# First value weights on ScalarE's DMA queue, norm rows in two tiles, constants after the first weights, rotary sines after the value projection

## The chip, the cores and the metric

The kernel runs on one core of a Trainium2 chip. The metric is the device time of one execution, in microseconds (us). The engines of the core run side by side and meet at semaphores: TensorE (PE), VectorE (DVE), ScalarE (ACT), GpSimd (POOL) and SyncE (SP, which here only starts DMA transfers). ScalarE and GpSimd can start DMA transfers too.

## What is computed

Two decoder layers over 256 positions of 1024 channels. Layer 0 mixes tokens by attention (8 heads of 128, rotary embedding on 32 of the 128 channels of a head, one block of 256 keys, so plain causal attention), layer 1 by causal pooling with windows 2, 4, 8 and 16. Each layer is followed by a squared-ReLU MLP of width 4096, and one RMSNorm ends the program. Cut to the part that the change touches:

```python
def rms_norm(x, g):
    return x * rsqrt(mean(x * x, axis=-1) + 1e-6) * g

xn = rms_norm(x, norm_mix[0])
q, k, v = split(xn @ w_qkv)                  # 8 heads of 128
q, k = rope(q, cos, sin), rope(k, cos, sin)  # on 32 of the 128 channels
p = softmax(q @ k.T / sqrt(128) + causal)
x = x + (p @ v) @ w_o
x = x + relu(rms_norm(x, norm_mlp[0]) @ w_up) ** 2 @ w_down
```

## The kernel before

All of x stays on the chip in `xt`. Every weight arrives as float32 in a slab of 1 MB (`raw_*`, three buffers) and is split into two parts, a high one (`wh_*`, ScalarE, L160) and the rest (`wl_*`, VectorE, L164); the activations are split likewise (`xs`, high half by ScalarE at L293, low half by VectorE at L299). A product is then three matmuls: high by high, low by high, high by low. A slab goes through the split in pieces of 512 or 1024 columns. The order of the engines' work is the order of the code: no scheduler moves anything. `pump(n)` writes n pieces of the next slab's split into the queues of ScalarE and VectorE at the place where it stands in the code; `use(...)` writes what is still missing of the slab that is needed. The load of a slab is issued on SyncE when the last piece of the slab three before it has been split (L167).

The start of the program, in the order in which TensorE sees it: eight matmuls on a zero tile (`warm`, L270, each recorded as two), the transposition of the 32 rows of the two norms' gains (`gps`, L274, copied to `gcol` by VectorE, L276), the transposition of the first 128 channels of x (`tr_a`, L287), two more zero matmuls, and then the value projection (`d_v`, L461), eight steps k of 12 matmuls with the transpositions of the later channels between them. Behind it come `rb` (L502), which spreads the inverse root mean square over the partitions, and four rounds j of: k projection (`u_k`), q projection (`u_q`), scores of the round before (`s`, L539 and L540), its softmax, its product with the values.

Beside that, GpSimd computes the rotary angles from the positions (L417 to L426, 18 instructions), VectorE brings them into range (`last_turn`, L429 to L432), ScalarE takes two sines (`sines`, L435 and L436, between two table loads), GpSimd forms the cosines (L438, L439), and VectorE multiplies both with `rb` into four tables (L508, L509). After each projection of round j VectorE swaps the rotary halves (`sw_k`, `sw_q`, L522) and multiplies by the cosines (`t_k`, `t_q`, L523), and GpSimd multiplies the swapped part by the sines (L524) and adds it (L525). The scores of a round wait for L525 of its q.

ScalarE's Sqrt of the mean square (`aerr`, L479) and VectorE's steps L482 to L491 behind it give `arst` and `diag`, which `rb` and the values' copies (`vsb`, L497) need. The queues of DMA: x and all weights on SyncE's; the two norms' rows (`grow`) on ScalarE's; `inv` and `pos_i`, which the rotary angles start from, on GpSimd's.

Of the kernel before, what the change touches and what calls it, by code (L numbers as in the profile page):

```python
# [11 lines left out]
F32 = mybir.dt.float32  # L12
# [29 lines left out]
N_WARM2 = 2  # L42
# [41 lines left out]
def tile_trunk(ctx: ExitStack, tc: tile.TileContext, x_in, positions, norm_mix, norm_mlp,  # L84
# [136 lines left out]
    tiny = cpool.tile([P, 1], F32, name="tiny")  # L221
    nc.scalar.activation(tiny, warm[:, 0:1], AF.Sqrt)
# [7 lines left out]
    grow = cpool.tile([32, P], F32, name="grow")  # L230
# [9 lines left out]
    def load_v0(eng, k, h):  # L240
        eng.dma_start(v0[:, k, h * HALF:(h + 1) * HALF], v0_src[:, k, h * HALF:(h + 1) * HALF])

    load_x(0, 1)
    nc.scalar.dma_start(grow[0:16, :], norm_mix.rearrange("l (k p) -> (l k) p", p=P))
    nc.scalar.dma_start(grow[16:32, :], norm_mlp.rearrange("l (k p) -> (l k) p", p=P))
    load_v0(nc.sync, 0, 0)
    load_v0(nc.sync, 0, 1)
    load_x(1, 1)
    load_v0(nc.sync, 1, 0)
    load_v0(nc.sync, 1, 1)  # L250
    load_x(2, 2)
    load_to(1)
    load_x(4, 4)
    inv = cpool.tile([ROT, 1], F32, name="inv")
    nc.gpsimd.dma_start(inv, consts[0:ROT, C_INV:C_INV + 1])
    pos_i = cpool.tile([ROT, SEQ], I32, name="pos_i")
    nc.gpsimd.dma_start(pos_i, positions.broadcast_to([ROT, SEQ]))
    cst = cpool.tile([P, C_ALL], F32, name="cst")
    load_to(RAW_BUFS - 1)
    nc.sync.dma_start(cst, consts)  # L260
# [12 lines left out]
    gps = ps_t.tile([P, HALF], F32, tag="t", name="gps")  # L273
    nc.tensor.transpose(gps[:, 0:32], grow, ident[0:32, 0:32])  # L274
    gcol = cpool.tile([P, 32], F32, name="gcol")
    nc.vector.tensor_copy(gcol, gps[:, 0:32])  # L276
# [167 lines left out]
    h, lo = transposes(0, 0, "a", n=1)  # L444
    keep_warm(N_WARM2)
# [4 lines left out]
    for k in range(KT):  # L450
# [12 lines left out]
        pump(2 if k < 3 or k == 6 else 1)  # L463
# [7 lines left out]
        if k == 6:  # L471
            sines()
        if k == 5:
            var0 = small.tile([P, NS], F32, tag="avar", name="avar", bufs=1)
            r0t = small.tile([P, NS], F32, tag="arst", name="arst", bufs=1)
            e0 = small.tile([P, NS], F32, tag="aerr", name="aerr", bufs=1)
            nc.vector.scalar_tensor_tensor(var0, acc0[:, 0, :], EPS, acc0[:, 1, :],
                                           op0=ALU.add, op1=ALU.add)
            nc.scalar.activation(e0, var0, AF.Sqrt)  # L479
            pump_h(1)  # L480
            last_turn()
            nc.vector.reciprocal(r0t, e0)  # L482
            nc.vector.tensor_tensor(e0, var0, r0t, op=ALU.mult)
            nc.vector.tensor_tensor(e0, e0, r0t, op=ALU.mult)
            nc.vector.tensor_scalar(e0, e0, -0.5, 1.5, op0=ALU.mult, op1=ALU.add)
            nc.vector.tensor_tensor(r0t, r0t, e0, op=ALU.mult)
            r0 = [r0t[:, s:s + 1] for s in range(NS)]
            diags = []
            for s in range(NS):
                diag = small.tile([P, P], F32, tag="diag%d" % s, name="diag%d" % s, bufs=1)  # L490
                nc.vector.tensor_scalar(diag, ident, r0[s], None, op0=ALU.mult)  # L491
                diags.append(diag)

# [11 lines left out]
    for nm, c in (("k", 1.0), ("q", scale)):  # L505
        ct = cpool.tile([P, 1, SEQ], F32, name="ct_" + nm)
        st = cpool.tile([ROT, 1, SEQ], F32, name="st_" + nm)
        nc.vector.scalar_tensor_tensor(ct[:, 0, :], rb[:, 0:SEQ], c, cos_t, op0=ALU.mult, op1=ALU.mult)  # L508
        nc.vector.scalar_tensor_tensor(st[:, 0, :], rb[0:ROT, 0:SEQ], c, sin_t, op0=ALU.mult, op1=ALU.mult)  # L509
        tab[nm] = (ct, st)  # L510
# [82 lines left out]
    for j in range(4):  # L593
# [12 lines left out]
        if j == 0:  # L606
            v_evac(0, 1)
            v_evac(1, 1)
        qk["k", j] = qk_evac("k", j, u)
# [365 lines left out]
```

## Time and profile before

| | before |
|---|---|
| median of 3 runs | 494.3 us (493.9 to 494.57) |
| the profiled execution, its own time | 494.89 us |
| its span in the profile | 493.1 us |
| TensorE matmul busy | 481.9 us, 98% of the span |
| VectorE, ScalarE, GpSimd busy | 333.1, 249.7, 50.2 us |

A row of the timeline gives the start and the length in us, the engine, the line, the operation, and what it writes and reads, with the count if rows were merged; in brackets stands how long the engine had been idle before it and what ended that. The records of neighbouring instructions on one engine overlap by up to 0.3 us, so what an instruction costs its engine is the distance from its start to the next start.

### The profile page before, as it was taken

How to read it: one execution, taken by the hardware profiler on the slowest of the kernel's cores; microseconds unless marked ns; L12 is line 12 of the kernel's file. 1: busy time of each engine (PE TensorE's matmuls, PEld its weight loads, DVE VectorE, ACT ScalarE, POOL GpSimd, SP SyncE). 2: the span in 40 equal slices, each digit the busy share in tenths (PEclk: the TensorE clock that was granted, in tenths of full speed). 3: DMA queues.
4: the chain of work that ended last, by engine and by line, in shares of the span. 5: the costliest groups of instructions: out<-in, count | busy, mean ns of one | idle time of the engine just before them, and what ended most of it. 6: DMA issues, size and time to landing. Idle time of an engine off the chain costs nothing.

```text
span 493.1 us, 6591 instructions
## 1 busy us (share of the span) xinstructions
PE 481.9 (98%) x2625; PEld 416.2 (84%) x2625; DVE 333.1 (68%) x484; ACT 249.7 (51%) x395; POOL 50.2 (10%) x46
## 2 busy tenths in 40 slices
PE   9999999999999999999999999999999999999993
PEld 7789899888888888888888889888888888888882
DVE  3788788765867866666666676678666666655645
ACT  4776444563665644444455553566444554445423
POOL 6935534200000000000000000000000000000000
PEclk9999999999999999999999999999999999999998
DMA  7949435471396656565554580077765555566102
GB/s 269 384 160 291 157 105 171 129 241 58 96 345 213 242 185 202 208 215 210 174 171 171 170 256 1 7 251 240 265 212 178 172 170 173 187 201 229 66 0 85
DMA packets 56078, 89.53 MB, mean 182 GB/s; under 512 B 1600, under 2 KB 44640, under 8 KB 56048
## 3 DMA queue, kind: packets, MB, share of 16 engines
q1 hardware_dynamic: 55632, 88.68, 53.8%
q8 instruction: 20, 0.33, 0.3%
q10 hardware_dynamic: 352, 0.41, 0.2%
q14 instruction: 10, 0.08, 0.0%
q0 software_dynamic: 64, 0.03, 0.0%
HBM read 88.06 MB, written 1.05 MB: 181 GB/s over the span
## 4 chain that ended last, share of the span: by engine, by line
PE 84%; POOL 5%; DVE 5%; ACT 2%; issue 2%; DMA 1%; POOLq 0%; ACTq 0%; DVEq 0%
PE u_m L381 24%; PE u_m L375 12%; PE d_m L352 11%; PE d_m L351 11%; PE d_m L353 11%; POOL rot_b L425 2%; PE d_o L353 1%; PE d_o L351 1%; PE d_o L352 1%; PE u_q L365 1%; PE u_q L360 1%; PE u_q L361 1%; POOL rot_a L426 1%; DMA raw_k<-in_attn_w_qkv_dram 1%; POOL sw_q L524 1%
## 5 line engine op out<-in xcount | busy, mean ns | idle before, releaser
L381 PE MATMUL u_m<-xs,wh_u 128*128 128x512 f32 x512 | 129.8, 395 | 0.0
L381 PEld LDWEIGHTS u_m<-xs,wh_u 128*128 128x128 f32 x512 | 91.8, 188 | 16.6
L352 PE MATMUL d_m<-wl_d,hh 128*128 128x512 f32 x256 | 99.9, 390 | 0.0
L351 PE MATMUL d_m<-wh_d,hh 128*128 128x512 f32 x256 | 99.9, 390 | 0.0
L353 PE MATMUL d_m<-wh_d,hl 128*128 128x512 f32 x256 | 99.6, 389 | 0.0
L164 DVE TENSOR_TENSOR wl_d<-raw_d,wh_d 128x1024 fp32r<-128x1024 f32 x64 | 77.8, 1224 | 23.3 <-ACT wh_d L160 23.3
L666 ACT ACTIVATE t<-u_m 128x256 f32<-128x256 f32 x64 | 24.4, 381 | 108.7 <-PE u_m L381 108.6
L164 DVE TENSOR_TENSOR wl_u<-raw_u,wh_u 128x1024 fp32r<-128x1024 f32 x64 | 75.5, 1219 | 1.8 <-ACT wh_u L160 1.8
L375 PEld LDWEIGHTS u_m<-xs,wl_u 128*128 128x128 f32 x512 | 70.0, 188 | 5.4
L375 PE MATMUL u_m<-xs,wl_u 128*128 128x256 f32 x512 | 72.7, 283 | 0.0
L160 ACT ACTIVATE wh_d<-raw_d 128x1024 fp32r<-128x1024 f32 x64 | 66.5, 1048 | 3.7 <-DMA raw_d<-in_mlp_w_down_dram 3.6
L667 DVE TENSOR_TENSOR t<-u_m,t 128x256 f32<-128x256 f32 x64 | 27.1, 424 | 56.8 <-ACT t L666 56.8
L160 ACT ACTIVATE wh_u<-raw_u 128x1024 fp32r<-128x1024 f32 x64 | 63.9, 1045 | 0.0
L351 PEld LDWEIGHTS d_m<-wh_d,hh 128*128 128x128 f32 x256 | 48.0, 188 | 10.6
L352 PEld LDWEIGHTS d_m<-wl_d,hh 128*128 128x128 f32 x256 | 48.1, 188 | 10.2
L353 PEld LDWEIGHTS d_m<-wh_d,hl 128*128 128x128 f32 x256 | 48.1, 188 | 10.2
L677 ACT ACTIVATE hh<-hf 128x512 fp32r<-128x512 f32 x32 | 20.2, 632 | 47.3 <-DVE hf L676 47.3
L678 DVE TENSOR_TENSOR hl<-hf,hh 128x512 fp32r<-128x512 f32 x32 | 22.2, 693 | 22.5 <-ACT hh L677 22.5
L676 DVE SCALAR_TENSOR_TENSOR hf<-t 128x512 f32<-128x512 f32 x32 | 22.2, 694 | 1.1
L360 PE MATMUL u_q<-xs,wh_q 128*128 128x256 f32 x64 | 18.6, 291 | 0.0
L360 PE MATMUL u_k<-xs,wh_k 128*128 128x256 f32 x64 | 18.5, 289 | 0.0
L365 PE MATMUL u_k<-xs,wh_k 128*128 128x256 f32 x64 | 18.1, 283 | 0.0
(170 smaller groups left out, 578.9 us busy)
## 6 DMA issues: line engine op xcount, KB each, us to landing
raw_u<-in_mlp_w_up_dram SPq DMA_DIRECT2D x32, 1024.0 KB, 5.8
raw_d<-in_mlp_w_down_dram SPq DMA_DIRECT2D x32, 1024.0 KB, 6.4
raw_k<-in_attn_w_qkv_dram SPq DMA_DIRECT2D x4, 1024.0 KB, 5.2
raw_q<-in_attn_w_qkv_dram SPq DMA_DIRECT2D x4, 1024.0 KB, 5.2
raw_o<-in_attn_w_o_dram SPq DMA_DIRECT2D x4, 1024.0 KB, 5.2
raw_v<-in_attn_w_qkv_dram SPq DMA_DIRECT2D x3, 1024.0 KB, 9.3
raw_v<-in_attn_w_qkv_dram SPq DMA_DIRECT2D x4, 256.0 KB, 4.4
pw<-in_pool_w_dram SPq DMA_DIRECT2D x1, 1024.0 KB, 11.2
```

Source lines behind the costliest of these rows:

```text
L160: nc.scalar.activation(wh[:, sl], src[:, sl], AF.Copy)
L164: nc.vector.tensor_tensor(wl[:, sl], src[:, sl], wh[:, sl].bitcast(F32), op=ALU.subtract)
L351: nc.tensor.matmul(acc, lh, wh, start=first, stop=False)
L352: nc.tensor.matmul(acc, lh, wl, start=False, stop=False)
L353: nc.tensor.matmul(acc, ll, wh, start=False, stop=last)
L360: nc.tensor.matmul(o, w[0][:, k, fs], hi, start=first, stop=False, skip_group_check=True)
L365: nc.tensor.matmul(acc[:, f * SEQ:(f + 1) * SEQ], w[0][:, k, fs], xs[:, k, SEQ:2 * SEQ], start=False, stop=last, skip_group_check=True)
L375: nc.tensor.matmul(acc[:, 0:SEQ], w[1][:, k, f * P:(f + 1) * P], xs[:, k, 0:SEQ], start=k == 0, stop=False, skip_group_check=True)
L381: nc.tensor.matmul(acc, w[0][:, k, f * P:(f + 1) * P], xs[:, k, :], start=False, stop=k == KT - 1, skip_group_check=True)
L666: nc.scalar.activation(t[:, ts], u[:, SEQ:2 * SEQ], AF.Copy)
L667: nc.vector.tensor_tensor(t[:, ts], u[:, 0:SEQ], t[:, ts], op=ALU.add)
L676: nc.vector.scalar_tensor_tensor(hf, t, 0.0, t, op0=ALU.max, op1=ALU.mult)
```

## The change

The first quarter of the first value slab is loaded over ScalarE's DMA queue, ahead of the gains; the second half of that slab is one transfer instead of two, and the second slab is two transfers of half a slab instead of one. The gains of the two norms lie in two tiles of 16 rows: `grow` (mixer norm) is transposed behind the first x transposition, `grow2` (MLP norm) inside the value projection. `inv` and `pos_i` come over ScalarE's queue instead of GpSimd's. ScalarE's first table load stands behind these four transfers. The constants (`cst`) are loaded behind the slab of `k` instead of behind the third slab. `N_WARM2` is 7 instead of 2. `last_turn` and `sines` stand behind the value projection instead of within its steps 5 and 6, the tables (`tables()`) behind the second half of the first k projection, and step 7 of the value projection pumps two pieces instead of one.

```diff
-N_WARM2 = 2
+N_WARM2 = 7
...
-    tiny = cpool.tile([P, 1], F32, name="tiny")
-    nc.scalar.activation(tiny, warm[:, 0:1], AF.Sqrt)
...
-    grow = cpool.tile([32, P], F32, name="grow")
+    grow = cpool.tile([16, P], F32, name="grow")
+    grow2 = cpool.tile([16, P], F32, name="grow2")
...
     load_x(0, 1)
-    nc.scalar.dma_start(grow[0:16, :], norm_mix.rearrange("l (k p) -> (l k) p", p=P))
-    nc.scalar.dma_start(grow[16:32, :], norm_mlp.rearrange("l (k p) -> (l k) p", p=P))
-    load_v0(nc.sync, 0, 0)
+    load_v0(nc.scalar, 0, 0)
+    nc.scalar.dma_start(grow, norm_mix.rearrange("l (k p) -> (l k) p", p=P))
     load_v0(nc.sync, 0, 1)
     load_x(1, 1)
-    load_v0(nc.sync, 1, 0)
-    load_v0(nc.sync, 1, 1)
+    nc.sync.dma_start(v0[:, 1, :], v0_src[:, 1, :])
     load_x(2, 2)
-    load_to(1)
+    raw1 = rawp.tile([P, SLAB], F32, tag="raw", name="raw_v_1")
+    raws[1] = raw1
+    state["raw"] = 2
+    for k in range(2):
+        nc.sync.dma_start(raw1[:, k * D:(k + 1) * D], slabs[1][1][:, k, :])
+    inv = cpool.tile([ROT, 1], F32, name="inv")
+    nc.scalar.dma_start(inv, consts[0:ROT, C_INV:C_INV + 1])
+    pos_i = cpool.tile([ROT, SEQ], I32, name="pos_i")
+    nc.scalar.dma_start(pos_i, positions.broadcast_to([ROT, SEQ]))
+    tiny = cpool.tile([P, 1], F32, name="tiny")
+    nc.scalar.activation(tiny, warm[:, 0:1], AF.Sqrt)
     load_x(4, 4)
...
+    nc.sync.dma_start(grow2, norm_mlp.rearrange("l (k p) -> (l k) p", p=P))
...
-    nc.sync.dma_start(cst, consts)
...
-    gps = ps_t.tile([P, HALF], F32, tag="t", name="gps")
-    nc.tensor.transpose(gps[:, 0:32], grow, ident[0:32, 0:32])
-    nc.vector.tensor_copy(gcol, gps[:, 0:32])
+    def gains(src, c0):
+        gps = ps_t.tile([P, HALF], F32, tag="t", name="gps_%d" % c0)
+        nc.tensor.transpose(gps[:, 0:16], src, ident[0:16, 0:16])
+        nc.vector.tensor_copy(gcol[:, c0:c0 + 16], gps[:, 0:16])
...
     h, lo = transposes(0, 0, "a", n=1)
+    gains(grow, 0)
     keep_warm(N_WARM2)
...
-        pump(2 if k < 3 or k == 6 else 1)
+        pump(2 if k < 3 or k >= 6 else 1)
+        if k == 2:
+            load_to(3)
+            nc.sync.dma_start(cst, consts)
+        if k == 6:
+            gains(grow2, 16)
...
-        if k == 6:
-            sines()
...
-            last_turn()
...
+    last_turn()
+    sines()
...
+    def tables():
...
             v_evac(1, 1)
+            tables()
```

TensorE's queue at the start, before; `warm_up` is the target of the zero matmuls, `gps` that of the gains' transposition:

```order
L270 MATMUL warm_up<-warm 128x128 x8
L274 MATMUL gps<-ident,grow 128x32
L287 MATMUL tr_a_158<-ident,xt 128x128 x2
L270 MATMUL warm_up<-warm 128x128 x2
L461 MATMUL d_v_153<-wh_v_163,xs 128x512
```

The same place after:

```order
L273 MATMUL warm_up<-warm 128x128 x8
L293 MATMUL tr_a_155<-ident,xt 128x128 x2
L281 MATMUL gps_158<-ident,grow 128x16
L273 MATMUL warm_up<-warm 128x128 x7
L468 MATMUL d_v_150<-wh_v_168,xs 128x512
```

Seven zero matmuls instead of two stand between the first transpositions and the first matmul of the value projection.

ScalarE's queue behind the split of the first k slab, before (`wh_q` is the first q slab, the last `wh_k` the second k slab):

```order
L160 ACTIVATE wh_k_344<-raw_k_237 128x1024 x2
L435 ACT_TABLE_LOAD
L435 ACTIVATE sin_t<-rot_a 32x256
L436 ACTIVATE rot_b<-rot_a 32x256
L437 ACT_TABLE_LOAD
L437 ACTIVATE tiny<-warm 128x1
L160 ACTIVATE wh_q_372<-raw_q_282 128x1024 x2
L160 ACTIVATE wh_k_419<-raw_k_348 128x1024
```

And after:

```order
L160 ACTIVATE wh_k_346<-raw_k_242 128x1024 x2
L160 ACTIVATE wh_q_372<-raw_q_288 128x1024 x2
L441 ACT_TABLE_LOAD
L441 ACTIVATE sin_t<-rot_a 32x256
L442 ACTIVATE rot_b<-rot_a 32x256
L443 ACT_TABLE_LOAD
L443 ACTIVATE tiny<-warm 128x1
L160 ACTIVATE wh_k_420<-raw_k_350 128x1024 x2
```

The sines have moved behind the first q slab, and directly behind them stands the second k slab, with both of its pieces.

VectorE's queue from the tables to the first round's q, before:

```order
L508 SCALAR_TENSOR_TENSOR ct_q<-rb,cos_t 128x256
L509 SCALAR_TENSOR_TENSOR st_q<-rb,sin_t 32x256
L164 TENSOR_TENSOR wl_q_373<-raw_q_282,wh_q_372 128x1024
L164 TENSOR_TENSOR wl_k_420<-raw_k_348,wh_k_419 128x1024
L522 STREAM_SHUFFLE sw_k_452<-u_k_390 32x512
L523 TENSOR_TENSOR t_k_451<-u_k_390,ct_k 128x512
L164 TENSOR_TENSOR wl_k_420<-raw_k_348,wh_k_419 128x1024
L164 TENSOR_TENSOR wl_q_462<-raw_q_353,wh_q_461 128x1024 x2
L522 STREAM_SHUFFLE sw_q_519<-u_q_465 32x512
```

After, from the last instruction of `last_turn` on:

```order
L438 TENSOR_SCALAR rot_a<-rot_a 32x256
L164 TENSOR_TENSOR wl_k_421<-raw_k_350,wh_k_420 128x1024 x2
L521 SCALAR_TENSOR_TENSOR ct_k<-rb,cos_t 128x256
L522 SCALAR_TENSOR_TENSOR st_k<-rb,sin_t 32x256
L521 SCALAR_TENSOR_TENSOR ct_q<-rb,cos_t 128x256
L522 SCALAR_TENSOR_TENSOR st_q<-rb,sin_t 32x256
L535 STREAM_SHUFFLE sw_k_465<-u_k_395 32x512
L536 TENSOR_TENSOR t_k_464<-u_k_395,ct_k 128x512
L164 TENSOR_TENSOR wl_q_471<-raw_q_355,wh_q_470 128x1024 x2
L164 TENSOR_TENSOR wl_k_504<-raw_k_378,wh_k_503 128x1024
L535 STREAM_SHUFFLE sw_q_532<-u_q_478 32x512
```

The whole first q slab and `last_turn` now stand ahead of the second k slab, the tables stand behind it, and one piece of the third k slab (`wl_k_504`) stands ahead of `sw_q`.

## Rows read from the trace of the kernel before

**Rows 1.** Waits of TensorE, whole span: for whom, us, times, longest.

```profile
PE s L539 <- POOL t_q L525: 1.1, 1, 1.1
```

**Rows 2.** Timeline of TensorE, start to the first scores.

```profile
1.05 3.78 PE L270 MATMUL warm_up<-warm 128*128 128x128 f32 x16 [1.05 <-DVE warm L220]
...
5.49 0.64 PE L270 MATMUL warm_up<-warm 128*128 128x128 f32 x4
6.25 1.25 PE L461 MATMUL d_v<-wh_v,xs 128*128 128x512 f32 x4
...
13.32 1.20 PE L461 MATMUL d_v<-wh_v,xs 128*128 128x512 f32 x4 [0.51 <-ACT xs L293]
...
16.74 0.60 PE L287 MATMUL tr_a<-ident,xt 128*128 128x128 f32 x4
17.09 2.10 PE L461 MATMUL d_v<-wh_v,xs 128*128 128x512 f32 x8
...
22.76 0.60 PE L287 MATMUL tr_a<-ident,xt 128*128 128x128 f32 x4
...
31.97 0.61 PE L502 MATMUL rb<-diag,ones 128*128 128x128 f32 x4
...
51.06 0.49 PE L539 MATMUL s<-t_k,t_q 128*128 128x128 f32 x2 [1.15 <-POOL t_q L525]
```

**Rows 3.** Timeline of ScalarE, first weights to the second k slab.

```profile
4.47 0.63 ACT L160 ACTIVATE wh_v<-raw_v 128x512 fp32r<-128x512 f32 x1 [2.24 <-DMA raw_v<-in_attn_w_qkv_dram]
...
25.29 0.20 ACT L479 ACTIVATE aerr<-avar 128x2 f32<-128x2 f32 x1 [0.45 <-DVE avar L477]
...
29.65 0.42 ACT L435 ACTIVATE sin_t<-rot_a 32x256 f32<-32x256 f32 x1
...
31.80 2.00 ACT L160 ACTIVATE wh_q<-raw_q 128x1024 fp32r<-128x1024 f32 x2
36.06 1.06 ACT L160 ACTIVATE wh_k<-raw_k 128x1024 fp32r<-128x1024 f32 x1 [2.27 <-DMA raw_k<-in_attn_w_qkv_dram]
```

**Rows 4.** Timeline of VectorE, mean square to the first round's q.

```profile
25.06 0.19 DVE L477 SCALAR_TENSOR_TENSOR avar<-acc 128x2 f32<-128x2 f32 x1
27.01 0.28 DVE L429 TENSOR_SCALAR rot_b<-rot_a 32x256 f32<-32x256 f32 x1 [1.76 <-POOL rot_a L426]
...
28.30 0.15 DVE L482 RECIPROCAL arst<-aerr 128x2 f32<-128x2 f32 x1
...
29.67 1.22 DVE L164 TENSOR_TENSOR wl_v<-raw_v,wh_v 128x1024 fp32r<-128x1024 f32 x1
...
33.70 1.21 DVE L164 TENSOR_TENSOR wl_q<-raw_q,wh_q 128x1024 fp32r<-128x1024 f32 x1
34.83 0.41 DVE L508 SCALAR_TENSOR_TENSOR ct_k<-rb,cos_t 128x256 f32<-128x256 f32 x1
...
36.16 1.20 DVE L164 TENSOR_TENSOR wl_q<-raw_q,wh_q 128x1024 fp32r<-128x1024 f32 x1
...
40.42 1.23 DVE L164 TENSOR_TENSOR wl_k<-raw_k,wh_k 128x1024 fp32r<-128x1024 f32 x1 [0.68 <-ACT wh_k L160]
41.56 3.46 DVE L164 TENSOR_TENSOR wl_q<-raw_q,wh_q 128x1024 fp32r<-128x1024 f32 x2
...
44.95 0.73 DVE L522 STREAM_SHUFFLE sw_q<-u_q 32x512 f32<-32x512 f32 x1
...
46.18 2.34 DVE L164 TENSOR_TENSOR wl_k<-raw_k,wh_k 128x1024 fp32r<-128x1024 f32 x2
```

**Rows 5.** Timeline of GpSimd, its share in the first and third round's q.

```profile
45.76 3.91 POOL L524 TENSOR_TENSOR sw_q<-sw_q,st_q 32x512 f32<-32x512 f32 x1 [2.96 <-DVE sw_q L522]
49.75 1.26 POOL L525 TENSOR_TENSOR t_q<-t_q,sw_q 32x512 f32<-32x512 f32 x1
...
74.63 1.28 POOL L524 TENSOR_TENSOR sw_q<-sw_q,st_q 32x512 f32<-32x512 f32 x1 [5.05 <-DVE sw_q L522]
```

**Rows 6.** Stretch around the wait at 51.06: us, busy by engine, PEclk, DMA share, GB/s.

```profile
49.00:51.10 2.10, 0.95 (x9) 0.75 (x7) 1.06 (x3) 0.00 (x0) 2.02 (x3) 1.00 0.78 235
```

More of the change, by code (lines that the diff above doesn't have):

```diff
@@ L243, in tile_trunk @@
     load_x(0, 1)
-    nc.scalar.dma_start(grow[0:16, :], norm_mix.rearrange("l (k p) -> (l k) p", p=P))
-    nc.scalar.dma_start(grow[16:32, :], norm_mlp.rearrange("l (k p) -> (l k) p", p=P))
-    load_v0(nc.sync, 0, 0)
+    load_v0(nc.scalar, 0, 0)
+    nc.scalar.dma_start(grow, norm_mix.rearrange("l (k p) -> (l k) p", p=P))
     load_v0(nc.sync, 0, 1)
     load_x(1, 1)
-    load_v0(nc.sync, 1, 0)
-    load_v0(nc.sync, 1, 1)
+    nc.sync.dma_start(v0[:, 1, :], v0_src[:, 1, :])
     load_x(2, 2)
-    load_to(1)
+    raw1 = rawp.tile([P, SLAB], F32, tag="raw", name="raw_v_1")
[9 more added lines that the diff above has]
+    nc.scalar.activation(tiny, warm[:, 0:1], AF.Sqrt)
     load_x(4, 4)
[L254 to L257, printed above, removed]
+    nc.sync.dma_start(grow2, norm_mlp.rearrange("l (k p) -> (l k) p", p=P))
     cst = cpool.tile([P, C_ALL], F32, name="cst")
     load_to(RAW_BUFS - 1)
-    nc.sync.dma_start(cst, consts)
     psb = cpool.tile([P, D], F32, tag="psb", name="psb")
@@ L504, in tile_trunk @@
     tab = {}
[L505 to L510, printed above, removed]
+    def tables():
+        for nm, c in (("k", 1.0), ("q", scale)):
+            ct = cpool.tile([P, 1, SEQ], F32, name="ct_" + nm)
+            st = cpool.tile([ROT, 1, SEQ], F32, name="st_" + nm)
+            nc.vector.scalar_tensor_tensor(ct[:, 0, :], rb[:, 0:SEQ], c, cos_t, op0=ALU.mult, op1=ALU.mult)
+            nc.vector.scalar_tensor_tensor(st[:, 0, :], rb[0:ROT, 0:SEQ], c, sin_t, op0=ALU.mult, op1=ALU.mult)
+            tab[nm] = (ct, st)
     swap = [(i + half) % ROT for i in range(ROT)]
```

## Prediction

> **What bounds the kernel now.** I read the waits of TensorE first, because it is the engine that is busy nearly all the time. There the reader is to see that in 493 us it waits only a few times, and longest, 1.1 us, for GpSimd's t_q ahead of the first scores [rows 1]. All that the change touches lies ahead of that point. So the question is when the first scores start: now at 51.06 us, 1.15 us after TensorE was ready at 49.91 [rows 2]. Behind it TensorE runs through to the last layer, so a shift of the first scores shifts the end by the same amount.
>
> Then I read the other engines backwards from 51.06, to see what sets t_q. GpSimd's t_q starts at 49.75 and follows its sw_q, which starts at 45.76 and takes 3.91 us, where the same instruction takes 1.28 in the third round [rows 5]. It can start when VectorE has made sw_q at 44.95 [rows 4]. VectorE is nearly always occupied from 25 to 48 us; its two large holes there are 1.76 us for GpSimd's angles ahead of last_turn, and 0.68 for ScalarE's wh_k [rows 4]. ScalarE in turn waited 2.27 us for the second k slab, until 36.06 [rows 3]. So the first scores hang on VectorE's and ScalarE's order, not on TensorE. A gain of TensorE alone is worth nothing until sw_q comes earlier too.
>
> **The start.** The first weights are there at 4.47 and the first product starts at 6.25 [rows 2, 3]: 1.78 us of slack. Loading them over ScalarE's queue can bring them a little forward, or, sharing the DMA engines with x, put them back; neither shows. The Trainium skill says as much ("DMA: Bandwidth & Descriptors", section "Issuing engines are not separate DMA queues"): transfers started by different engines run on the same DMA engines, and only issue time is saved. No row here tests that yet.
>
> What counts is the five more zero matmuls, two passes each. Sixteen passes took from 1.05 to about 4.77, 0.23 us each, at the lower clock; the four at 5.49 took 0.64 together, 0.16 each with the last one's end, and a transposition, a pass of the same shape, takes (17.09 − 16.74) / 4 = 0.09 later on [rows 2]. Ten more passes at 0.11, between 0.09 and 0.16, are 1.1 us; at 0.23 they would be 2.3. I take 1.1, as the pace has already doubled at 5.49. They end at 6.13 + 1.1, so the first product starts at 7.2 instead of 6.25, 0.95 later.
>
> What that buys: two steps with one group of four transpositions take 22.76 − 16.74 = 6.02 us without waits [rows 2]. Four transpositions cost 0.35, so a step is 2.83. From 6.25 to 16.74 lie three steps, two transpositions and one group of four: 3 × 2.83 + 0.22 + 0.35 = 9.06. They took 10.49, so some 1.42 us are waits (the 0.51 in brackets at 13.32 is part of them). With half of the second slab landing on its own, and a later start, I let all 1.42 vanish: 0.95 − 1.42 = −0.47. The transpositions at 22.76 come at 22.29. The later steps, one transposition of grow2 (0.11) and no wait in step 7 (VectorE's last value piece is ready early, below) give rb at 22.29 + 0.35 + 3 × 2.83 + 0.11 = 31.24 instead of 31.97. TensorE is then ready for the scores at 49.91 − 0.73 = 49.2. More than 51.06 − 49.2 = 1.9 us cannot be won.
>
> **VectorE, ScalarE, VectorE.** The chain goes step by step, from rows 3 and 4 throughout.
> - avar, which waits for the last transpositions: 25.06 − 0.47 = 24.6. ScalarE's aerr ends 0.43 behind it, so the reciprocal starts at 25.05. Here last_turn and its 1.76 us of waiting are gone.
> - From the reciprocal to the next split piece: 29.67 − 28.30 = 1.37, so wl_v at 26.4.
> - Five pieces (the last value piece, two of k, two of q) at 34.83 − 33.70 = 1.13 are 5.65; the copy of the second gains some 0.2: last_turn at 32.3. Its length is 28.30 − 27.01 = 1.29: 33.6.
> - ScalarE has split the q slab by about 30 and stands idle until 33.6. The sines and the table load behind them take 31.80 − 29.65 = 2.15: 35.75. Then comes wh_k, 1.06: 36.8. It had started at 36.06; its slab is now requested some 3 us sooner, so the load is hidden, but the sines have taken its place.
> - VectorE stands idle from 33.6 to 36.8. Then two k pieces 2.26, the tables 36.16 − 34.83 = 1.33, sw_k and t_k as long as sw_q and t_q, 46.18 − 44.95 = 1.23: 41.65.
> - Two q pieces, at least 2.26. Before they took 44.95 − 41.56 = 3.39, because GpSimd's t_k ran in between. GpSimd has sw_k to do at the same moment now, so I take 3.39 and keep 2.26 as the lower end: 45.05.
> - One piece of the third k slab, new ahead of sw_q: 1.13. So sw_q at 46.2 instead of 44.95.
> - From sw_q to the scores: 51.06 − 44.95 = 6.11 with GpSimd's sw_q at 3.91. Two ready pieces still follow t_q directly, as at 46.18, so I take the same: first scores at 52.3.
>
> That is 1.2 us later than 51.06, and TensorE waits about 3 us there instead of 1.15. Of what is removed (1.76 + 0.68 + 0.47, and the wait for the k slab), the idle 3.2 us, the extra piece and the second gains take back more. The profiled execution took 494.89, so it would take 496.1; it stands 0.6 above the median of 494.3, so I forecast 495.5 us.
>
> The rest costs nothing: cst is needed at 52 us and now lands behind a slab that was read at 26; inv and pos_i feed angles that are not waited for any more; tables() behind the k projection is in the chain above; the tail is untouched.
>
> **Rivals.**
> - The shared work of VectorE and GpSimd falls out a little better: sw_q of GpSimd or the two q pieces lose one piece's length less (1.13). First scores at 51.2, time 494.4. For it: 3.39 was one chance encounter. Against it: the same two kinds of instruction meet at the same place.
> - GpSimd runs freely. Its sw_q starts 0.42 us before VectorE's piece at 46.18 and yet takes 3.91; but at 74.63 it takes 1.28 [rows 4, 5]. If both q steps run at 1.28 and 1.26, the scores follow sw_q by 0.8 + 1.28 + 0.08 + 1.26 = 3.45: 49.7, time 493.0. The Trainium skill ("SBUF — State Buffer", section "Who interferes with whom") speaks for this one: whoever of the two starts first keeps the shared port for its whole instruction. By that sw_q, starting first, would have ended at 47.05; the row at 45.76 disagrees, the one at 74.63 agrees.
> - The longer wait lets the clock fall. The 1.15 us wait left it at 1.00 [rows 6]; this one is 3. After the first matmul at 1.05 the passes ran at half pace until about 5.5 [rows 2]; the same again would cost half of 4.4, so 2.2 more: 497.7. This one decides only if the first scores come after about 52. The Trainium skill ("TensorE: Matmul & The Clock Gate", section "Why this matters for your kernels") warns of idle gaps of TensorE between bursts of matmuls; no row here shows such a fall in the middle.
> - The start does not do what it says: half a slab lands no earlier and half of the 1.42 us of waits stay, behind a start 0.95 later. Then everything from the last transpositions on is 0.7 later: 496.2.
>
> **How the numbers follow.** A measurement of this kernel can tell about 0.2%, 1.0 us, from no change: below 493.3 is faster, above 495.3 slower. Chances: forecast 0.43 (495.5, of which 0.31 above 495.3 and 0.12 below), the better meeting 0.25 (494.4; 0.22 same, 0.03 faster), GpSimd free 0.18 (493.0; 0.17 faster, 0.01 same), the clock 0.06 (slower), the start 0.08 (slower). That gives faster 0.20, same 0.35, slower 0.45. For 8 times in 10 the range goes from 492.8 (GpSimd free, a little better still; 492.4 is the floor) to 497.0 (the bad start, with one piece of the q steps held a little longer; the clock case stays outside). Cases of both signs hold much of the chance; the forecast's own range is 494.9 to 496.3, from the row durations above with the start half a us either way.
>
> **What would show it right or wrong.** First product near 7.2; no waits at steps 2 and 7; rb near 31.2. ScalarE idle some 3.5 us ahead of the first sine, and VectorE some 3 ahead of the second k slab. sw_q near 46.2, the first scores near 52.3 behind a TensorE wait of 3 us. If that wait is under 1.5 us, or GpSimd's first sw_q takes 1.3, the forecast is too late; if passes after it run at 0.23, the clock fell.

## Result, and the profile after the change

The changed kernel takes 499.43 us (median of four executions, 498.55 to 499.99) where the kernel before took 494.35 in the same comparison: a ratio of 1.0101, with a 95% interval of 1.0089 to 1.0113. The forecast was 495.5 and its range ended at 497.0; the direction was right, the loss was four times as large as foretold.

The profiled execution took 499.21 us, with a span of 496.9; before it was 494.89 and 493.1. Its 4.32 us lie in three places. Up to the first scores: 52.52 instead of 51.06, 1.46 later. From the first scores to the end of the span: 496.9 − 52.52 = 444.38 instead of 493.1 − 51.06 = 442.04, 2.34 more. Outside the span: 2.31 instead of 1.79, 0.52 more. The rest of the 5.08 us between the medians is where the two profiled executions stand among their kind (0.54 above the median before, 0.22 below it after).

Waits of TensorE in the changed kernel (for whom, us, times, longest). Besides that for its first operand this is the only one left, and it has grown from the 1.1 us of [rows 1]:

```profile
PE s L552 <- POOL t_q L538: 4.2, 1, 4.2
```

Timeline of TensorE in the changed kernel, to be held against [rows 2] (start, length, instructions, and in brackets the idle time ahead with what ended it):

```profile
4.78 1.83 PE L273 MATMUL warm_up<-warm 128*128 128x128 f32 x14
6.36 1.17 PE L468 MATMUL d_v<-wh_v,xs 128*128 128x512 f32 x4
...
21.52 0.60 PE L293 MATMUL tr_a<-ident,xt 128*128 128x128 f32 x4
...
30.66 0.61 PE L513 MATMUL rb<-diag,ones 128*128 128x128 f32 x4
...
52.52 0.80 PE L552 MATMUL s<-t_k,t_q 128*128 128x128 f32 x2 [4.15 <-POOL t_q L538]
```

From the first product to rb no bracket is left: 30.66 − 6.36 = 24.30, where it was 31.97 − 6.25 = 25.72. TensorE is ready for the scores 1.5 us sooner, at 52.52 − 4.15 = 48.37, and then stands. The first two score matmuls take 0.80 together instead of 0.49. The stretches show why (us, busy time by engine, granted clock, DMA share, GB/s):

```profile
48.00:52.00 4.00, 0.36 (x4) 0.15 (x2) 2.08 (x4) 0.00 (x0) 3.92 (x3) 0.96 0.91 284
52.00:58.00 6.00, 5.48 (x21) 5.12 (x22) 2.58 (x10) 1.63 (x7) 2.95 (x3) 0.50 0.07 24
```

TensorE worked 0.36 us of the four before 52, the granted clock began to fall inside that wait (0.96 over these four), and over the six us behind it the clock was 0.50, the 1.2 GHz level. In [rows 6], around the shorter wait, it had stayed at 1.00, and so it had behind that wait, over the same six us of the kernel before:

```profile
52.00:58.00 6.00, 6.00 (x51) 5.95 (x51) 5.00 (x16) 2.82 (x9) 1.51 (x2) 1.00 0.19 65
```

VectorE in the changed kernel, from its idle time to the first round's q (compare [rows 4]):

```profile
36.96 2.36 DVE L164 TENSOR_TENSOR wl_k<-raw_k,wh_k 128x1024 fp32r<-128x1024 f32 x2 [3.26 <-ACT wh_k L160]
39.24 0.41 DVE L521 SCALAR_TENSOR_TENSOR ct_k<-rb,cos_t 128x256 f32<-128x256 f32 x1
...
40.58 0.73 DVE L535 STREAM_SHUFFLE sw_k<-u_k 32x512 f32<-32x512 f32 x1
41.22 0.66 DVE L536 TENSOR_TENSOR t_k<-u_k,ct_k 128x512 f32<-128x512 f32 x1
41.81 2.34 DVE L164 TENSOR_TENSOR wl_q<-raw_q,wh_q 128x1024 fp32r<-128x1024 f32 x2
44.07 1.21 DVE L164 TENSOR_TENSOR wl_k<-raw_k,wh_k 128x1024 fp32r<-128x1024 f32 x1
...
45.22 0.74 DVE L535 STREAM_SHUFFLE sw_q<-u_q 32x512 f32<-32x512 f32 x1
45.86 0.66 DVE L536 TENSOR_TENSOR t_q<-u_q,ct_q 128x512 f32<-128x512 f32 x1
46.45 1.20 DVE L164 TENSOR_TENSOR wl_k<-raw_k,wh_k 128x1024 fp32r<-128x1024 f32 x1
47.58 1.21 DVE L164 TENSOR_TENSOR wl_q<-raw_q,wh_q 128x1024 fp32r<-128x1024 f32 x1
```

GpSimd in the same stretch (compare [rows 5]):

```profile
41.40 5.04 POOL L537 TENSOR_TENSOR sw_k<-sw_k,st_k 32x512 f32<-32x512 f32 x1 [5.76 <-DVE sw_k L535]
46.52 3.39 POOL L538 TENSOR_TENSOR t_k<-t_k,sw_k 32x512 f32<-32x512 f32 x1
49.88 1.26 POOL L537 TENSOR_TENSOR sw_q<-sw_q,st_q 32x512 f32<-32x512 f32 x1
51.21 1.25 POOL L538 TENSOR_TENSOR t_q<-t_q,sw_q 32x512 f32<-32x512 f32 x1
```

These two lists are to be read together. GpSimd's sw_k starts at 41.40 and ends at 46.44, 1.16 us after the last of three split pieces that VectorE runs without a gap (44.07 + 1.21 = 45.28). Its t_k ends at 49.91, 1.12 after the next two (48.79). A step of GpSimd that meets no piece takes 1.25 to 1.3. So while VectorE's pieces follow one another, GpSimd gets nowhere, and when they end it still needs 1.12 to 1.16 us, nearly its own length. Before, a whole row of pieces held GpSimd once, at sw_q: 49.67, 1.15 after the pieces from 46.18 ended at 48.52. Two steps of GpSimd then stood behind VectorE's last piece (the rest of sw_q, and t_q); now three do.

### The profile page after: what moved, and what is told of

Same layout as the page of the kernel before. It is cut to its first block, busy times and chain, and to the rows that moved or that the text cites. A ratio compares the mean times of both kernels' runs of the same rounds, so it can differ in the third digit from the quotient of the medians.

```text
span 496.9 us, 6612 instructions
## 1 busy us (share of the span) xinstructions
PE 484.2 (97%) x2636; PEld 419.5 (84%) x2636; DVE 332.5 (67%) x485; ACT 249.2 (50%) x395; POOL 49.0 (10%) x44
## 4 chain that ended last, share of the span: by engine, by line
PE 88%; DVE 7%; ACT 2%; issue 2%; POOL 1%; ACTq 0%; DVEq 0%
PE u_m L387 24%; PE u_m L381 12%; PE d_m L358 11%; PE d_m L357 11%; PE d_m L359 11%; PE d_v L468 3%; PE d_o L357 1%; PE d_o L359 1%; PE d_o L358 1%; PE u_q L366 1%; PE u_q L367 1%; PE u_q L371 1%; PE warm_up L273 1%; DVE wl_k L164 1%; PE s L553 1%
## 5 line engine op out<-in xcount | busy, mean ns | idle before, releaser
L366 PE MATMUL u_q<-xs,wh_q 128*128 128x256 f32 x64 | 19.5, 304 | 0.0
L367 PE MATMUL u_q<-xs,wl_q 128*128 128x256 f32 x64 | 18.7, 292 | 0.0
L371 PE MATMUL u_q<-xs,wh_q 128*128 128x256 f32 x64 | 18.7, 292 | 0.0
```

Source lines behind the costliest of these rows:

```text
L366: nc.tensor.matmul(o, w[0][:, k, fs], hi, start=first, stop=False, skip_group_check=True)
L367: nc.tensor.matmul(o, w[1][:, k, fs], hi, start=False, stop=False, skip_group_check=True)
L371: nc.tensor.matmul(acc[:, f * SEQ:(f + 1) * SEQ], w[0][:, k, fs], xs[:, k, SEQ:2 * SEQ], start=False, stop=last, skip_group_check=True)
```

## Experiments

The theory to test was the prediction's own: the sines' new place leaves ScalarE and VectorE idle, the first scores come late, TensorE waits, and, as the trace now says, its clock falls. Against it stood: the start's edits cost; the extra split piece costs; and it is not VectorE's lateness but GpSimd being held by VectorE that makes t_q late.

What was measured, with the ratio to the kernel before on the same chip and its 95% interval, and from the profiled execution the first product, the first scores, TensorE's wait there and the length of GpSimd's first sw_k:

| kernel | us | ratio | first product | first scores | wait | sw_k |
|---|---|---|---|---|---|---|
| b_start | 494.40 | 1.0014 [1.0003, 1.0024] | 6.48 | 49.88 | 1.37 | 1.28 |
| b_start_tab | 494.85 | 1.0018 [1.0009, 1.0028] | 6.95 | 50.68 | 1.69 | 5.03 |
| a_pump7 | 496.36 | 1.0046 [1.0031, 1.0061] | 7.55 | 51.89 | 2.33 | 5.03 |
| changed | 499.43 | 1.0101 [1.0089, 1.0113] | 6.36 | 52.52 | 4.15 | 5.04 |
| a_sines_back | 496.18 | 1.0047 [1.0029, 1.0065] | 7.32 | 52.20 | 2.89 | 5.02 |
| b_sines | 497.17 | 1.0059 [1.0039, 1.0078] | 6.13 | 52.40 | 2.55 | 5.04 |
| a_fill | 496.55 | 1.0054 [1.0033, 1.0075] | 6.89 | 52.79 | 0 | 5.04 |
| a_dve_rot | 494.39 | 1.0011 [1.0000, 1.0022] | 7.80 | 50.37 | 0.53 | on VectorE |
| b_dve | 493.08 | 0.9982 [0.9971, 0.9993] | 5.71 | 49.44 | 0 | on VectorE |
| b_start_dve | 492.29 | 0.9965 [0.9954, 0.9976] | 7.21 | 49.03 | 0 | on VectorE |
| b_dve_warm2 | 492.22 | 0.9964 [0.9950, 0.9978] | 6.25 | 48.85 | 0 | on VectorE |

The first four rows are a ladder: each has all edits of the row above it and one more (the start; the tables; the sines; the extra piece).

**The start alone.** The kernel before with all edits of the change but the sines, the tables and the extra piece; two of them for example:

```diff
-N_WARM2 = 2
+N_WARM2 = 7
...
-    load_v0(nc.sync, 0, 0)
+    load_v0(nc.scalar, 0, 0)
```

> The kernel before with the start's edits alone: first weights on ScalarE's queue, norm rows split, constants later, seven zero matmuls instead of two. Sines, tables and pumps as before. Theory (the sines' place decides): no loss, first scores within 0.5 us of 51.06, 493.8 to 494.8; the waits in steps 0 to 2 are gone, rb 1 us sooner, and TensorE's wait ahead of the scores longer by about as much, 2 to 2.7 us, clock at 1.00. Rival (the start's edits cost by the queues or by the longer wait that a faster TensorE runs into): 497 or more, with the clock at half behind the wait.

It came out at 494.40, in the theory's range, with the clock at 1.00. The first scores (49.88, so 1.18 us sooner and not within half a us) and the wait (1.37, not 2 to 2.7) are not as foretold, but these 1.18 us are hardly a gain of the kernel: its profiled execution, at 493.79 us, is the fastest of ten, and that of the kernel before stands 0.54 above its median. By the ratio the start alone costs 0.7 us, of which half a us lies outside the span (below). It is not what costs the 5 us.

**The tables behind the k projection**, on top of the start:

```diff
+    def tables():
...
         if j == 0:
             v_evac(0, 1)
             v_evac(1, 1)
+            tables()
```

> The kernel before with the start's edits and with the four tables made behind the k projection, just ahead of sw_k; sines and pumps as before. With the start alone GpSimd's sw_k started at 38.12 and took 1.28 us. Theory (the tables' place delays sw_k by up to 1.33 us on VectorE, past the hole in which GpSimd gets in, so that its sw_k is held by the split pieces): GpSimd's sw_k near 5 us, first scores 1 to 1.5 us later against the first product, 495.5 to 496.3. Rival (the tables' place costs nothing): GpSimd's sw_k 1.28, 494.0 to 494.7.

The mechanism was right, the price wrong: 494.85 lies between the two ranges. VectorE with the start alone, and GpSimd:

```profile
39.27 1.23 DVE L164 TENSOR_TENSOR wl_k<-raw_k,wh_k 128x1024 fp32r<-128x1024 f32 x1 [0.67 <-ACT wh_k L160]
40.42 3.44 DVE L164 TENSOR_TENSOR wl_q<-raw_q,wh_q 128x1024 fp32r<-128x1024 f32 x2
```

```profile
38.12 1.28 POOL L537 TENSOR_TENSOR sw_k<-sw_k,st_k 32x512 f32<-32x512 f32 x1 [6.64 <-DVE sw_k L535]
39.48 2.15 POOL L538 TENSOR_TENSOR t_k<-t_k,sw_k 32x512 f32<-32x512 f32 x1
```

and with the tables moved, VectorE, then GpSimd:

```profile
39.73 1.20 DVE L164 TENSOR_TENSOR wl_k<-raw_k,wh_k 128x1024 fp32r<-128x1024 f32 x1
40.86 2.34 DVE L164 TENSOR_TENSOR wl_q<-raw_q,wh_q 128x1024 fp32r<-128x1024 f32 x2
```

```profile
39.31 5.03 POOL L538 TENSOR_TENSOR sw_k<-sw_k,st_k 32x512 f32<-32x512 f32 x1 [6.75 <-DVE sw_k L536]
44.43 3.63 POOL L539 TENSOR_TENSOR t_k<-t_k,sw_k 32x512 f32<-32x512 f32 x1
```

In the first pair VectorE stands idle for 0.67 us ahead of wl_k, and GpSimd's sw_k, which begins 1.15 us ahead of the piece, runs through in 1.28. In the second there is no bracket ahead of wl_k, three pieces follow without a gap, and sw_k takes 3.75 us longer. By the ratios the time rose by only some 0.2 us, and the intervals overlap; what was foretold was 1 to 1.5. The reading of the rows is that VectorE's two q pieces are no longer held in turn (2.34 instead of 3.44), so that sw_q comes no later.

**The sines as well**: the changed kernel without its extra split step.

```diff
-        pump(2 if k < 3 or k >= 6 else 1)
+        pump(2 if k < 3 or k == 6 else 1)
```

> The changed kernel with one split step in step 7 of the value projection, as before, instead of two: one piece of the third k slab fewer ahead of sw_q; all else stays. Theory (the extra piece holds GpSimd's sw_k and moves sw_q by its 1.13 us): sw_q near 44.1, GpSimd's sw_k near 3.9, first scores near 51.4 and a wait of 3 us; 497 to 498.3, or 495.5 to 496.5 where the clock stands that wait. Rival (the piece only changes places): first scores 52.5, 499 or more.

496.36 lies in the second of the two ranges. By the ratios the sines' place costs 1.4 us on top of b_start_tab, and the extra piece 2.7 on top of that, most of which is the longer wait's clock (2.3 by the ratios, see the filled wait below). But sw_k was not 3.9: three pieces stand behind t_k here too, and it took 5.03. In the profiled execution the clock stood the wait of 2.33 us. The four executions had mean clocks of 0.998, 0.998, 0.991 and 0.992, at 495.85, 495.95, 496.77 and 496.91 us: at this length it seems to fall in some and not in others. (The mean takes in the end of the span, where TensorE has stopped; b_dve, with no wait at the scores, has 0.994 in its profiled execution. So a mean is a hint; only for the profiled execution do rows show that the clock stood.)

**The sines back in steps 5 and 6**, the rest of the change kept:

```diff
+        if k == 6:
+            sines()
...
+            last_turn()
...
-    last_turn()
-    sines()
```

> The changed kernel with last_turn back in step 5 and sines() back in step 6 of the value projection; its start, its extra pump in step 7 and its late tables() stay. Theory (the sines' place behind the values leaves ScalarE 2.06 us and VectorE 3.26 us idle, and with that TensorE waits 4.15 us and its clock falls): the two idles vanish, the first scores come at or before 51.3, the granted clock stays at 1.00 over 50 to 60 us, and the time is 493.5 to 495.0 instead of 499.4. Rival (the start's queues and loads, or the extra piece of the third k slab ahead of sw_q, cost the time): 498 or more.

A miss: the time lies between the two ranges. VectorE's idle time ahead of the k pieces is smaller (1.20 instead of 3.26), yet the first scores come at 52.20 and the time is 496.18. The theory that the sines' place decides is too narrow: with late tables and one more piece GpSimd's sw_k is held for 5.02 us here as well. What the time gets back, 2.7 us by the ratios, is not much more than the clock alone is worth in the changed kernel (2.3), and the clock stood here.

**The sines and tables alone**, in the kernel before:

```diff
-        if k == 6:
-            sines()
...
-            last_turn()
...
+    last_turn()
+    sines()
...
+    def tables():
...
+            tables()
```

> The kernel before with only last_turn and sines() moved behind the value projection and the four tables behind the k projection; start and pumps as before. Theory: VectorE and ScalarE idle as in the changed kernel, the first scores come 1 to 2 us later than 51.06; as TensorE is ready only at 49.9, its wait is 2.2 to 3.2 us; 495.5 to 496.5 if the clock stands that, 498 if it falls. So the clock needs both parts if 495.5 to 496.5 comes out. Rival (the sines cost nothing, the loss is the start's): 494.0 to 494.8.

497.17. The first scores were as foretold (52.40), and the clock did not need both parts: in the profiled execution (497.79) it fell behind a wait of 2.55 us, shorter than the 2.89 of a_sines_back, where it did not. The six executions fall into two of 495.17 and 495.90, with mean clocks of 0.997 and 0.998, and four of 497.10 to 497.79, with 0.991 to 0.994, so here too it seems to fall in some only. The waits, and the stretch behind them, of b_sines:

```profile
PE s L539 <- POOL t_q L525: 2.6, 1, 2.6
```

```profile
52.00:58.00 6.00, 5.60 (x30) 5.31 (x31) 3.03 (x13) 2.37 (x9) 2.82 (x3) 0.72 0.20 66
```

and of a_sines_back:

```profile
PE s L553 <- POOL t_q L539: 2.9, 1, 2.9
```

```profile
52.00:58.00 6.00, 5.80 (x45) 5.70 (x46) 3.96 (x16) 2.82 (x9) 2.65 (x3) 1.00 0.14 28
```

So the length of the wait alone does not tell whether it falls.

**The wait filled.** The changed kernel, with TensorE busy ahead of the first scores:

```diff
+N_FILL = 18
...
+        if j == 0:
+            fill = ps_d.tile([P, HALF], F32, tag="d00", name="fill")
+            for i in range(N_FILL):
+                nc.tensor.matmul(fill[:, 0:P], warm, warm, start=True, stop=True)
```

> The changed kernel with 18 zero matmuls (128x128, two passes each, about 0.22 us) ahead of the first scores, into a bank of the value projection that has been read: TensorE works through its 4.15 us of waiting, nothing else is moved. Theory (about 2.4 us of the loss is the fall of the clock behind the wait): the granted clock stays at 1.00 over 50 to 60 us, first scores at 52.5 as before, time 496.5 to 497.3 instead of 499.4. Rival (the clock falls for another reason, or its fall costs nothing since VectorE and ScalarE set the pace there): 499 or more.

TensorE, and the two stretches of before:

```profile
48.77 4.18 PE L551 MATMUL fill<-warm 128*128 128x128 f32 x36
52.79 0.39 PE L557 MATMUL s<-t_k,t_q 128*128 128x128 f32 x2
```

```profile
48.00:52.00 4.00, 4.00 (x37) 4.00 (x37) 2.23 (x4) 0.00 (x0) 3.92 (x3) 1.00 0.95 308
52.00:58.00 6.00, 6.00 (x50) 5.90 (x49) 3.46 (x14) 2.73 (x9) 3.13 (x3) 1.00 0.17 25
```

The scores come no sooner, the clock is 1.00, and the time is 496.55, 2.9 us less (2.3 by the ratios). From the first scores to the end of the span it is 494.4 − 52.79 = 441.6 instead of 444.4. That shows the fall of the clock and its price, 2.8 us in these profiles.

**Round 0's rotary steps on VectorE**, in the changed kernel:

```diff
-        nc.gpsimd.tensor_tensor(sw, sw, st.broadcast_to([ROT, 2, SEQ]), op=ALU.mult)
-        nc.gpsimd.tensor_tensor(t[0:ROT], t[0:ROT], sw, op=ALU.add)
+        e = nc.vector if j == 0 else nc.gpsimd
+        e.tensor_tensor(sw, sw, st.broadcast_to([ROT, 2, SEQ]), op=ALU.mult)
+        e.tensor_tensor(t[0:ROT], t[0:ROT], sw, op=ALU.add)
```

> The changed kernel with round 0's four rotary steps (sw times sine, t plus sw, for k and for q) on VectorE instead of GpSimd; all else stays. Theory (GpSimd's sw_k, 5.04 us, and t_k, 3.39, are held while VectorE's split pieces run back to back, and that, more than VectorE's own lateness, makes t_q late): at some 0.65 us each VectorE gets 2.6 us more work, sw_q starts near 46.5, the first scores near 49.2, TensorE's wait about 0.8, the granted clock 1.00 over 50 to 60 us, time 493.5 to 495. Rival (VectorE's idle 3.26 us and the sines' place alone set it; GpSimd's share is its own length): VectorE only gets later, first scores at 52 or more, 498.5 or more.

VectorE in this kernel, whose first product is 1.44 us later than that of the changed one's profile:

```profile
42.99 0.67 DVE L538 TENSOR_TENSOR sw_k<-sw_k,st_k 32x512 f32<-32x512 f32 x1
43.69 0.68 DVE L539 TENSOR_TENSOR t_k<-t_k,sw_k 32x512 f32<-32x512 f32 x1
44.30 2.34 DVE L164 TENSOR_TENSOR wl_q<-raw_q,wh_q 128x1024 fp32r<-128x1024 f32 x2
...
49.64 0.68 DVE L539 TENSOR_TENSOR t_q<-t_q,sw_q 32x512 f32<-32x512 f32 x1
```

Four steps of 0.67 us replace GpSimd's 5.04, 3.39, 1.26 and 1.25. VectorE's own idle 3.26 us is still there (3.25), and still the wait is 0.53 and the time 494.39, 5.0 us less than the changed kernel's (4.4 by the ratios). Counted from the first product, the scores come at 42.57 instead of 46.16. So the theory of this run holds: what made the scores late is GpSimd, held by VectorE. The time also holds what follows from the shorter wait, the clock (2.3 by the ratios), and half a us outside the span (about 1.8 instead of 2.27).

**The same edit in the kernel before, without and with the start.**

> The kernel before with round 0's four rotary steps on VectorE, nothing else. Theory (port): GpSimd's sw_q, 3.91 us there, is what the 1.15 us wait ahead of the first scores hangs on; the wait goes, first scores at 49.9, 492.5 to 493.3 where before gives 494.1. Rival (VectorE is late by the 2.6 us that it takes over): 494 or more.

> The kernel before with the start's edits, and round 0's four rotary steps on VectorE. With the start alone the first scores came at 49.88 behind a wait of 1.37, with GpSimd's sw_q at 3.89. Theory (port): the scores are ready when TensorE is, at about 48.5; no wait; span 490.0 to 490.5 and, with the 2.28 us that lie outside the span with this start, 492.2 to 493.0. Rival (VectorE becomes late by the 2.6 us it takes over): first scores at 50 or later, 494.4 or more.

493.08 and 492.29, both in the range of the theory of the held GpSimd. (In the second the time outside the span is 1.8 us and not the 2.28 foretold.) The wait ahead of the first scores is gone in both, so these 1.15 us of the kernel before were the same thing. b_start_dve beats both kernels, by 0.35% the one before and by about 7 us the changed one. With two zero matmuls instead of seven:

```diff
-N_WARM2 = 7
+N_WARM2 = 2
```

> The kernel before with the start's edits and round 0's rotary steps on VectorE (492.3 us), but with two zero matmuls ahead of the first product, as before, instead of seven. Theory (the waits of 1.42 us in steps 0 to 2 go because the second slab's halves and the rest come sooner): no waits, first product 1.1 us sooner or more, 490.8 to 491.5. Rival (they go because TensorE starts later): the waits come back, by about as much, 492 to 492.6; or the clock rises later and it is slower still.

TensorE in this kernel:

```profile
6.25 1.26 PE L468 MATMUL d_v<-wh_v,xs 128*128 128x512 f32 x4
...
31.26 0.60 PE L514 MATMUL rb<-diag,ones 128*128 128x128 f32 x4
```

492.22, the rival's range: in the profiled execution TensorE starts 0.96 us sooner than in that of b_start_dve, and from the first product to rb it takes 31.26 − 6.25 = 25.01 us, halfway between 25.72 and 24.30. So in this pair about half of the removed waits goes with the sooner loads, the other half with the later start; it is one execution of each, and the first product alone came at 6.36 to 7.80 in the profiles with seven zero matmuls. By the medians the five zero matmuls neither cost nor gain.

**Outside the span.** In the first runs the time stood 2.23 to 2.35 us over the span in every execution with the changed start, and 1.74 to 1.86 in the others (spans are on record to 0.1 us, so each of these is good to 0.05). Four kernels asked why. Two are the start alone, with ScalarE's first table load ahead of its loads again (s_tiny), or with the two small loads on GpSimd's queue again (s_pool):

```diff
+    tiny = cpool.tile([P, 1], F32, name="tiny")
+    nc.scalar.activation(tiny, warm[:, 0:1], AF.Sqrt)
     ident = cpool.tile([P, P], F32, name="ident")
...
-    tiny = cpool.tile([P, 1], F32, name="tiny")
-    nc.scalar.activation(tiny, warm[:, 0:1], AF.Sqrt)
     load_x(4, 4)
```

```diff
-    nc.scalar.dma_start(inv, consts[0:ROT, C_INV:C_INV + 1])
+    nc.gpsimd.dma_start(inv, consts[0:ROT, C_INV:C_INV + 1])
...
-    nc.scalar.dma_start(pos_i, positions.broadcast_to([ROT, SEQ]))
+    nc.gpsimd.dma_start(pos_i, positions.broadcast_to([ROT, SEQ]))
```

> The kernel before with the start's edits, but with the tiny activation (and with it ScalarE's first table load) ahead of ScalarE's DMA issues, as in the kernel before. With this start the time stood 2.23 to 2.35 us over the span in ten executions, before 1.74 to 1.86 in fifteen. Theory A (where the first table load stands makes the 0.5 us): 1.80. Theory B (the constants' loads that left GpSimd's queue, or something else of the start): 2.28.

> The kernel before with the start's edits, but with the loads of inv and pos_i on GpSimd's queue, as in the kernel before. Theory B (the 0.5 us outside the span come from taking these two loads off GpSimd's queue): the time stands 1.80 over the span. Theory A (the first table load's place): 2.28.

s_tiny stands 2.28 over its span, s_pool 1.83. That spoke for the loads, but a_dve_rot, with the loads on ScalarE's queue, stands at 1.78 to 1.88. What goes with the two levels in all kernels is the number of GpSimd's instructions. So the changed kernel was given two more of them, and the kernel before two fewer, by the second of the edits above turned round:

```diff
+    pad = cpool.tile([P, 1], F32, name="pad")
+    nc.gpsimd.memset(pad, 0.0)
+    nc.gpsimd.memset(pad, 1.0)
```

> The changed kernel with two more small memsets (128x1) on GpSimd in its start, so that GpSimd has 46 instructions in the profile as before instead of 44; nothing depends on them. So far the time stood 2.23 to 2.35 us over the span with 44 GpSimd instructions, 1.74 to 1.88 with 46 or 40, and between them with 42. Theory (it goes with GpSimd's instruction stream, not with a queue): 1.80 over the span, time 498.9. Rival (the constants' loads on ScalarE's queue make it): 2.28, 499.4.

> The kernel before with the loads of inv and pos_i on ScalarE's queue instead of GpSimd's, nothing else: 44 GpSimd instructions in the profile. Theory (GpSimd's instruction stream): 2.28 over the span. Rival (something else of the start): 1.80.

The first section of the page (busy us, share, instructions), of the changed kernel and of a_pool2:

```profile
PE 484.2 (97%) x2636; PEld 419.5 (84%) x2636; DVE 332.5 (67%) x485; ACT 249.2 (50%) x395; POOL 49.0 (10%) x44
```

```profile
PE 483.8 (97%) x2636; PEld 418.5 (84%) x2636; DVE 331.3 (67%) x485; ACT 249.2 (50%) x395; POOL 49.3 (10%) x46
```

With 44 it is 2.23 to 2.35 in all eight kernels, with 46 or 40 it is 1.74 to 1.88 in seven, with 42 (b_dve) 1.82 to 2.19. a_pool2, which only adds two memsets, stands at 1.75 and 1.81 and takes 498.53 (1.0099 [1.0063, 1.0135], two executions: beside the 1.0101 of the changed kernel the time itself shows no gain clear of noise); b_act_consts, with 44, stands at 2.24 to 2.35 and takes 495.56 (1.0033 [1.0017, 1.0050]; it also waits 2.7 us for ScalarE's xs in the first steps, and its sw_k is held for 5.03 us though its tables stand as before). So the 0.5 us follow GpSimd's instruction stream, not the queue; fewer instructions are not simply worse, since 40 is as good as 46. Why is open.

## Why the prediction was wrong, point by point

- **The start** (first product at 7.2, all 1.42 us of waits gone). From the first product to rb 25.72 − 24.30 = 1.42 us are gone, but not quite where the working had them: up to the last transpositions 16.51 became 21.52 − 6.36 = 15.16, so 1.35 less, and from there to rb it takes 9.14 where the working had 8.95. The first product came at 6.36 in the changed kernel's profile, but at 6.36 to 7.80 in the eleven profiles with seven zero matmuls, 7.06 in the middle; 7.2 was fair for the kernel and 0.8 too late for this execution. So TensorE was ready at 48.37 instead of 49.2, which only made the wait longer.
- **VectorE and ScalarE to sw_k.** Right to 0.2 us from the first split piece on: wl_v 26.60 (26.4), last_turn 32.36 (32.3), the idle time up to 36.96 (36.8), t_k done by 41.81 (41.65). Ahead of it two errors cancel, in part by luck: the reciprocal came at 24.61 instead of 25.05, since TensorE was early, and from it to wl_v it took 1.99 instead of 1.37.

```profile
24.61 0.17 DVE L491 RECIPROCAL arst<-aerr 128x2 f32<-128x2 f32 x1 [0.27 <-ACT aerr L489]
...
26.60 1.22 DVE L164 TENSOR_TENSOR wl_v<-raw_v,wh_v 128x1024 fp32r<-128x1024 f32 x1
...
32.36 0.27 DVE L435 TENSOR_SCALAR rot_b<-rot_a 32x256 f32<-32x256 f32 x1
```

ScalarE's side of it is sin_t behind last_turn and wh_k behind the second table load. Its idle time ahead of the sine is 2.06 instead of some 3.5, as the first table load falls into it:

```profile
30.40 1.28 ACT L441 ACT_TABLE_LOAD   x1
33.74 0.42 ACT L441 ACTIVATE sin_t<-rot_a 32x256 f32<-32x256 f32 x1 [2.06 <-DVE rot_a L438]
...
35.89 2.00 ACT L160 ACTIVATE wh_k<-raw_k 128x1024 fp32r<-128x1024 f32 x2
```

- **Two q pieces, 3.39.** Wrong: they took 44.07 − 41.81 = 2.26, the lower end that the prediction kept. In [rows 4] GpSimd had got in between them; here it was GpSimd that was held. So sw_q came at 45.22, not 46.2. The extra piece was right (1.15 against 1.13).
- **From sw_q to the scores, 6.11.** The step that failed in the chain: 7.30. The 6.11 held for a GpSimd that is done with k when sw_q comes. Here it still had the end of sw_k and all of t_k ahead of it. The two errors cancel, 52.52 against 52.3, so the sum looked right for a wrong reason; a_dve_rot showed that the term that matters is GpSimd's; in b_start_tab the hold came when VectorE's hole behind t_k was filled.
- **The rival "GpSimd runs freely".** Half of it came: sw_q and t_q took 1.26 and 1.25. But they ran behind sw_k and t_k. The Trainium skill ("SBUF — State Buffer", section "Who interferes with whom") has whoever issues first keep the pair of ports. By that sw_k, starting 0.41 us ahead of wl_q at 41.81, would have ended near 42.7; the trace disagrees, and so it does in the other five kernels of the table with an sw_k of 5.02 to 5.04, where it starts 0.40 to 0.41 ahead. But rows of later rounds agree: in a_dve_rot a sw_q that starts as far ahead, 0.41, runs through in 1.28, and VectorE's piece takes 1.96 instead of 1.2. So which of the two is held is not settled by these starts.

```profile
61.01 1.28 POOL L538 TENSOR_TENSOR sw_q<-sw_q,st_q 32x512 f32<-32x512 f32 x1 [5.05 <-DVE sw_q L535]
```

```profile
61.42 1.96 DVE L164 TENSOR_TENSOR wl_k<-raw_k,wh_k 128x1024 fp32r<-128x1024 f32 x1
```

The same section says that a VectorE step with at most one input in SBUF, outside its two-port modes, does not contend. That the trace bears out: sw_k ended at 46.44, during VectorE's t_q, which reads u_q in PSUM and one table in SBUF.
- **The clock.** The step that failed in the sum. The prediction wrote that this rival decides if the scores come after about 52, forecast 52.3, and yet gave it 0.06. With a wait of 4.15 us the clock fell to 1.2 GHz, and that cost 2.8 us in the profiles, 2.3 by the ratios (a_fill). The price of 2.2 was near; what failed is that it was left out of the sum and of the range. The Trainium skill's warning ("TensorE: Matmul & The Clock Gate", section "Why this matters for your kernels") of idle gaps between bursts of matmuls is borne out in the middle of the kernel.
- **Outside the span.** Taken as unchanged; it was 0.5 more. The working's "The rest costs nothing", which takes in the loads of inv and pos_i, was wrong, though not through the transfers: GpSimd had two instructions fewer, and with two others in their place (a_pool2) the 0.5 us were gone.

With 1.46, 2.34 and 0.52 us, the forecast held 1.2 of the first and nothing of the other two.

## What to carry to other kernels

Before costing a step that GpSimd and VectorE share, list what VectorE has ready behind it: a hole in VectorE's row may be what lets GpSimd run, and filling it, or queueing one more piece, can cost several times the piece. Where a forecast says that TensorE will wait longer than it did in any row, the fall of its clock belongs in the main sum, with its price, and not among the small rivals. A short step that TensorE waits for was better put here on the engine that produces its input, though that engine is the busier one: in all three kernels in which it was tried, the time fell.

## What was not expected of the hardware

- In round 0 of twelve profiles 25 of GpSimd's 32x512 steps were held by VectorE's 128x1024 pieces, and every one ended 1.12 to 1.16 us after the end of a piece. 19 of them began between 0.43 us ahead of a piece's start and 0.07 behind it, and were held to the end of the whole gapless row, two or three pieces. The other 6 began 0.21 us or more behind a piece's start, and were let in after that piece; where a further piece followed, that one was held (t_k at 39.48 in b_start, 0.21 behind wl_k's start at 39.27).
- Later rounds show the other outcomes. A sw_q that begins 0.58 to 0.70 ahead of a piece, with 0.10 us or more of idle time on VectorE in front of the piece, takes 1.27 to 1.30, and the piece takes 1.68 to 1.79 instead of 1.2. A t_q that begins 0.08 to 0.10 behind a piece's start is let in after that one piece. And the sw_q of a_dve_rot shown above runs through from 0.41 ahead, with no idle time in front of the piece. So the start alone does not decide; what does is open.
- TensorE's clock stood waits of 1.15, 1.37, 1.69, 2.33 and 2.89 us in the profiled executions and fell behind those of 2.55, 3.77 (a_pool2: 0.72 over 52 to 58 us) and 4.15.
- Two small instructions on GpSimd, with nothing depending on them, took half a us off the time outside the span (2.25 to 2.31 before, 1.75 and 1.81 with them).
